# A transformer block on one core: the bias table's loads, its product and the pieces of one weight block are moved and recut

## The chip, the core and the metric

The kernel runs on one core of a Trainium2 chip. A core has five engines that run their own instruction streams and meet at semaphores: TensorE (PE, matrix products; its weight loads are listed as PEld), VectorE (DVE), ScalarE (ACT), GpSimd (POOL) and SyncE (SP). Data move between the memory outside the core and its own memory through 16 DMA engines. A transfer is issued by an instruction on SP, ACT or POOL. The metric is the time of one execution in device microseconds; the kernel before took 297.29 us (median of 3, 296.46 to 297.39).

## What is computed

One block for 256 tokens of width 1024, all in 32-bit floats:

```python
u = rms_norm(h, mix_norm_g[l])
proj = u @ w_in[l]
q, k, v, glu_a, glu_g = jnp.split(proj, splits, axis=-1)
attn_out = moba_attention(heads(q), heads(k), heads(v), rel_bias)
conv_out = conformer_conv(glu_a, glu_g, conv_w[l], conv_b[l], conv_ln_g[l], conv_ln_b[l])
mixed = jnp.concatenate([attn_out, conv_out], axis=-1)
h = h + mixed @ w_out[l]
u = rms_norm(h, ffn_norm_g[l])
h = h + (jax.nn.silu(u @ w_gate[l]) * (u @ w_up[l])) @ w_down[l]
return rms_norm(h, final_norm_g)
```

With 256 tokens there is one attention block of 256 keys, so attention is causal over all tokens, with 8 heads of 64. To each score a bias is added that depends on the head and on the distance of query and key: `rel_bias` is a table of 32 rows (buckets of distance) by 8 heads, and keys ahead of the query are masked. This bias is what the change is about.

## The kernel before

**Products in split parts.** Each 32-bit weight is split into an upper part `wh` (rounded to the matmul's fast 32-bit type, F32R) and a lower part `wl` (the raw value less `wh`); activations likewise. A product is three matmuls: upper by upper, upper by lower, lower by upper (`mm3`, `a_mm`). The upper part is made by `high` (ACT, or DVE for the pieces in `COPY_V`), the lower by `split` (DVE). Raw weights arrive in `raw` buffers of 128x1024, six in all, two to a block; `load` issues their DMAs on SP, one for each piece that `pieces` gives: halves of a block (1024 columns), or quarters (512 columns) for names in `FINE` (L37).

**Order.** All engines run in the order in which the program is traced (`keep_in_program_order`). Most of the first two thirds is a hand-written list, `PROGRAM` (L43 to L53), of steps that the table `ops` maps to functions. An engine's order is the order in which the steps give it instructions; where an instruction must wait, all behind it on that engine wait.

**Start.** Before the list runs, SP issues eight chunk pairs (L197 to L199): a 128x512 piece of the first weight block (`raw_a`, blocks `a0_0`, `a0_4`) and a 128x256 chunk of x (`xs`). POOL sets `ones`, issues the DMAs of the one-hot matrix `hot_s` and of the bias table `rbt` (L201, L202), sets constants, and issues the DMA of the late columns of the vector table `pv` (L216, taps of the convolution, not read before the convolution's weights are made). PE runs nine matmuls on `ones` to warm up.

**First products.** Steps `a0.0` to `a0.7` each take one chunk: ACT and DVE make `wh`, the two parts `us` of x, and `wl`, and PE runs 12 matmuls into `pa` and `pg`. Then `a1.0` to `a1.3` take the weight blocks `a1_0` and `a1_1`, two chunks each. Meanwhile `sq.*` adds up the squares of x (`accx`), `rs` turns them into the norm's factor (PE `ps_x`, DVE `ms_x`, POOL `rc_x`, DVE `dg_x`), and `rb` spreads it over the columns (PE `pb_x`). `glu.0` makes the convolution's input `upad`; `ud.0` writes it out (POOL), `us.0` reads it back four times, shifted (`ustk`, SP), for the matmuls `c.0.0` (`pc`).

**The bias.** `hot` is 33x384: for each of 384 distances a one-hot column (scaled) or, for masked ones, the 33rd row with the mask's value; `rbt` has the table in 32 rows and ones in the 33rd. `pz` (`bias_mm`, after `a0.0` in the list) multiplies them in plain F32 into 8x384, `zs` (ACT) copies the result out, `zd` (POOL) writes it to memory outside the core, and `bd` (SP, after `ld.qk1`) reads it into `bias`, each partition one column further on. The first reader is step `t.0` (`lg` on DVE).

Of the kernel before, what the change touches and what calls it, by code (L numbers as in the profile page):

```python
# [10 lines left out]
F32 = mybir.dt.float32  # L11
F32R = mybir.dt.float32r
# [17 lines left out]
MASK = 1e30  # L30
ZN = 384
# [2 lines left out]
ONV = TAPS - 4 * Q  # L34
UW = S + 32
LOOK = 2
FINE = ("a0_0", "a0_4")  # L37
COPY_V = (("a0_0", 0), ("a0_0", 1))
WARM = 9
SHIFT = 16  # L40
MIX = 48

PROGRAM = """  # L43
ld.a1_0 a0.0 pz a0.1 a0.2 a0.3 zs zd ld.a1_1 a0.4 a0.5 a0.6 a0.7 ld.qk0
w.a1_0.0 sq.0 sq.1 w.a1_0.1 sq.2 sq.3 sq.4 ld.qk1 bd a1.0 w.a1_1.0 sq.5 sq.6 sq.7 h.a1_1.1 h.qk0.0 h.qk0.1 a1.1 rs
w.a1_1.1 w.qk0.0 ld.qk2 a1.2 rb glu.0 ud.0 w.qk0.1 ld.v0 us.0 a1.3 w.qk1.0 w.qk1.1 glu.1 ud.1 us.1 ld.qk3
qk.0.0 qk.0.1 qo.0 cw.0 h.qk2.0 h.qk2.1 qk.1.0 sc.0 qk.1.1 w.qk2.0 t.0 w.qk2.1 ct.0.0.1 ld.v1 qo.1 c.0.0 h.v0.0 n.0 ct.0.1.3 sc.1 t.1 h.v0.1 ct.0.3.4 w.v0.0
c.0.1 fl.0 fo.0 n.1 h.qk3.0 ct.0.4.5 w.v0.1 w.qk3.0 qk.2.0 fl.1 fo.1 qk.2.1 ld.o0 ct.0.5.7 qo.2 h.qk3.1
v.0 cw.1 w.qk3.1 ld.o1 sc.2 t.2 v.1 h.v1.0 co.0 w.v1.0 qk.3.0 n.2 h.v1.1 w.v1.1 ld.o2 ct.1.0.2 fl.2 fo.2 qk.3.1 h.o0.0 w.o0.0 qo.3
# [5 lines left out]
PV_G1, PV_G2, PV_CB, PV_LG, PV_LB, PV_T = 0, 8, 16, 20, 24, 28  # L55
PV_CW = PV_T + CC * ONV
PV_FOLD = PV_CW + 16 * Q
PV_N = PV_FOLD + 32
# [3 lines left out]
def block_kernel(ctx, tc, xT, w_in, w_out, w_gu, w_down, pvec, gfin, relb, hot, out):  # L62
    nc = tc.nc
    const = ctx.enter_context(tc.tile_pool(name="const", bufs=1))
# [4 lines left out]
    w1 = ph1.enter_context(tc.tile_pool(name="w1", bufs=1))  # L69
# [3 lines left out]
    def mm(*args, **kw):  # L73
        return tc.keep_in_program_order(nc.tensor.matmul(*args, **kw))  # L74
# [12 lines left out]
    act, vec, pool, sync = (InOrder(e) for e in (nc.scalar, nc.vector, nc.gpsimd, nc.sync))  # L87

    def bank(i, name):
        return psum.tile([P, 512], F32, tag=f"b{i}", name=name)  # L90
# [86 lines left out]
    us = const.tile([P, KD * 2 * S + SHIFT], F32R, name="us")  # L177
# [3 lines left out]
    pv = const.tile([P, PV_N + 8], F32, name="pv")  # L181
# [2 lines left out]
    ident = const.tile([P, P], F32, name="ident")  # L184
    warm = const.tile([P, 1], F32, name="warm")
    accx = w1.tile([P, S], F32, name="accx")
    rbt = w1.tile([NB + 1, 32], F32, name="rbt")
    hot_s = w1.tile([NB + 1, ZN], F32, name="hot_s", tag="lg", bufs=2)
    upad = [w1.tile([P, 2 * UW + 4], F32, name=f"upad{i}", tag="pts", bufs=4) for i in range(2)]
    ustk = []  # L190
    wstk = [w1.tile([P, 8 * Q, 32], F32, name=f"wstk{i}", tag="wstk", bufs=2) for i in range(2)]
# [5 lines left out]
    for k in range(KD):  # L197
        next(first[k // 4])
        sync.dma_start(xs[:, k], xT[:, k * S : (k + 1) * S])  # L199
    pool.memset(ones, 1.0)  # L200
    pool.dma_start(hot_s, hot)  # L201
    pool.dma_start(rbt[0:NB, 0:H], relb)  # L202
    wm = bank(4, "wm")
    for i in range(WARM):
        mm(wm[:, 0:P], ones, ones, start=i == 0, stop=i == WARM - 1)
# [1 line left out]
    pool.affine_select(out=ident, in_=ident, compare_op=ALU.not_equal, fill=1.0, base=0,  # L207
                       pattern=[[-1, P]], channel_multiplier=1)
    pool.memset(mhalf, -0.5)
    pool.memset(rbt[NB : NB + 1, 0:H], 1.0)  # L210
    for t in upad:
        pool.memset(t[:, 0 : TAPS - 1], 0.0)
        pool.memset(t[:, TAPS - 1 + S : UW + TAPS - 1], 0.0)
        pool.memset(t[:, UW + TAPS - 1 + S :], 0.0)
    pool.memset(invc, 1.0 / (CC * P))
    pool.dma_start(pv[:, PV_T:PV_N], pvec[:, PV_T:])  # L216

    col = lambda lo, i: pv[:, lo + i : lo + i + 1]

# [66 lines left out]
    ud = [dram.tile([P, 2 * UW + 4], F32, name=f"ud{half}") for half in range(2)]  # L286
# [59 lines left out]
    rb = w1.tile([P, S], F32, name="rb")  # L346
# [3 lines left out]
        act.copy(rb, pb[:, :S])  # L350


    zs = w1.tile([H, ZN], F32, name="zs", tag="lg", bufs=2)
    zd = dram.tile([H, ZN], F32, name="zd")
    bias = w1.tile([P, H, S], F32, name="bias")

# [3 lines left out]

    pzs = []

    def bias_mm():
        pzs.append(bank(6, "pz"))
        mm(pzs[0][0:H, 0:ZN], rbt[:, 0:H], hot_s, start=True, stop=True)

    def bias_copy():
        act.copy(zs, pzs[0][0:H, 0:ZN])

    def bias_out():  # L370
        pool.dma_start(zd, zs)
# [161 lines left out]
    def a0(k):  # L533
# [3 lines left out]
        split(f"a0_{k // 4 * 4}", k % 4)  # L537
        a_mm(0, k, f"a0_{k // 4 * 4}", k % 4 * 512)

    ops = {"ld": fetch, "zd": bias_out, "bd": bias_in, "ud": stack_out, "us": stack_in, "h": high, "w": split, "rb": row_scale, "pz": bias_mm, "zs": bias_copy, "vt": v_out, "rs": scale_x,  # L540
           "a0": a0, "a1": a1, "glu": glu, "qk": qk_mm, "qo": qk_out, "sc": score, "t": logits, "n": normed, "fl": flip,
           "fo": flip_out, "v": v_mm, "pv": pv_mm, "mo": mix_out, "l": norm, "o": o_mm, "f": finish, "c": conv,
           "co": conv_out, "cw": conv_weights, "ct": conv_taps, "hs": lambda m: sumsq(acch, xs[:, m], m, "h"),
# [83 lines left out]
    hb = w2.tile([P, KD, KD, 32], F32, name="hb")  # L627
# [57 lines left out]
    a, b = FG - 2, FG - 1  # L685
    for t in range(2):
# [32 lines left out]
        sq = w2.tile([P, 512], F32, name=f"fsq{t}2", tag="fsq", bufs=2)  # L719
# [13 lines left out]
def _buckets():  # L733
    half = NB // 2
    d = np.arange(S)
    large = half + (np.log(np.maximum(d, 1) / half) / math.log(128 / half) * (NB - half) + 1e-9).astype(int)
    return np.where(d < half, d, np.minimum(large, NB - 1))


def _one_hot():  # L740
    hot = np.zeros((NB + 1, ZN), np.float32)
    b = _buckets()
    for n in range(ZN):
        dist = n - (P - 1)
        if 0 <= dist < S:
            hot[b[dist], n] = float(HD) ** 0.5
        else:
            hot[NB, n] = -MASK
    return hot

# [20 lines left out]
def _layout(x, mix_norm_g, w_in, rel_bias, conv_w, conv_b, conv_ln_g, conv_ln_b, w_out,  # L773
            ffn_norm_g, w_gate, w_up, w_down, final_norm_g):
    flat = lambda a: np.ascontiguousarray(a.reshape(P, -1))
    wi = _rows_d(w_in[0])
    q, k, v, a, g = (wi[:, :, i * 512 : (i + 1) * 512] for i in range(5))
    parts = []
    for half in range(2):
        c = slice(half * S, (half + 1) * S)  # L780
        parts.append(np.concatenate([a[:, :, c], g[:, :, c]], axis=2).reshape(P, -1))
    for hp in range(4):
        c = slice(hp * P, (hp + 1) * P)
        parts.append(np.concatenate([q[:, :, c], k[:, :, c]], axis=2).reshape(P, -1))
# [34 lines left out]
```

## Time and profile before

| what | value |
|---|---|
| three runs | 297.29 us median, 296.46 to 297.39 |
| the profiled execution | 296.92 us, of which the profile's span covers 295.0 |
| DVE, ACT, POOL busy | 203.3, 149.2, 44.2 us |
| DMA | 63.73 MB, mean 216 GB/s over the span |
| SP's own DMA queue (q1) | 54.80 MB, 57.2% of 16 engines |
| POOL's DMA queue (q0) | 8.08 MB, 9.7% |

The span runs from the first to the last instruction that the profile lists. "Busy" is the time in which an engine had at least one instruction under way. The chain of work that ended last is followed back from the last instruction; a step on it that gets shorter makes the kernel shorter, unless another chain is nearly as long. q1 is fed by SP and q0 by POOL; both end on the same 16 DMA engines, so the share of one is taken from what is left to the other.

### The profile page before, as it was taken

The numbers are of one execution on the slowest core, as the hardware profiler recorded it, in microseconds if no ns is written. First come the engines' busy times: TensorE is split into PE (matmuls) and PEld (weight loads), VectorE is DVE, ScalarE is ACT, GpSimd is POOL, SyncE is SP. The second block draws the span as 40 slices with busy tenths as digits, with TensorE's granted clock in tenths as the row PEclk, the third lists the DMA queues.
The fourth block names the chain that finished last, engine by engine and source line by source line (L and its number), as shares of the span: only waits on it lengthen the run. The fifth ranks groups of instructions, "written<-read, shape, count | busy, mean of one in ns | idle before, by whom it ended". The sixth has DMA issues, their size and how long they took to land.

```text
span 295.0 us, 4763 instructions
## 1 busy us (share of the span) xinstructions
PE 286.6 (97%) x1750; PEld 243.3 (82%) x1750; DVE 203.3 (69%) x373; ACT 149.2 (51%) x251; POOL 44.2 (15%) x83
## 2 busy tenths in 40 slices
PE   8999999999999999999999999999999999999991
PEld 6899987887689998888888888888888888888880
DVE  2887999888988689864975748282838466321894
ACT  2984554364583778634645454361718163402531
POOL 4000000000000000232231313321411313130000
PEclk9999999999999999999999999999999999999997
DMA  6999879945317455886998939979795959420022
GB/s 188 353 396 345 266 168 267 364 103 189 81 65 244 143 184 154 280 327 208 304 348 213 315 139 299 326 224 367 241 268 158 303 126 321 147 71 1 0 69 76
DMA packets 21624, 63.73 MB, mean 216 GB/s; under 512 B 3117, under 2 KB 5701, under 8 KB 21600
## 3 DMA queue, kind: packets, MB, share of 16 engines
q1 hardware_dynamic: 18176, 54.80, 57.2%
q0 software_dynamic: 2992, 8.08, 9.7%
q10 hardware_dynamic: 432, 0.54, 0.5%
q8 instruction: 14, 0.23, 0.3%
q14 instruction: 10, 0.08, 0.1%
HBM read 58.08 MB, written 5.32 MB: 215 GB/s over the span
## 4 chain that ended last, share of the span: by engine, by line
PE 92%; issue 2%; DMA 2%; DVE 2%; SPq 1%; ACT 0%; POOLq 0%; POOL 0%; DVEq 0%
PE pf L74 41%; PE pd L74 18%; PE pqk L74 8%; PE py L74 7%; PE pv L74 4%; PE pc L74 4%; PE pa L74 3%; PE pg L74 3%; DMA raw_a<-in_w_in 2%; PE pt L77 1%; PE ps L74 1%; PE po L74 1%; DVE ht L85 1%; SPq L85 1%; DVE hg L85 0%
## 5 line engine op out<-in xcount | busy, mean ns | idle before, releaser
L74 PE MATMUL pf<-wl,us 128*128 128x512 f32 x176 | 68.5, 389 | 0.0
L74 PE MATMUL pf<-wh_u,us 128*128 128x512 f32 x176 | 56.3, 390 | 0.0
L74 PE MATMUL pf<-wh_g,us 128*128 128x512 f32 x176 | 56.0, 389 | 0.0
L85 DVE TENSOR_TENSOR ff<-fs,pf 128x256 f32<-128x256 f32 x22 | 9.0, 418 | 53.0 <-ACT fs L85 53.0
L85 ACT ACTIVATE fs<-pf,rc_h 128x256 f32<-128x256 f32 x22 | 10.3, 474 | 65.2 <-PE pf L74 64.7
L74 PEld LDWEIGHTS pf<-wh_u,us 128*128 128x128 f32 x176 | 33.0, 188 | 6.9
L74 PEld LDWEIGHTS pf<-wh_g,us 128*128 128x128 f32 x176 | 33.0, 188 | 6.9
L74 PEld LDWEIGHTS pf<-wl,us 128*128 128x128 f32 x176 | 33.0, 188 | 6.7
L74 PE MATMUL pd<-wh_d,fh 128*128 128x512 f32 x84 | 32.9, 391 | 0.0
L74 PE MATMUL pd<-wh_d,fl 128*128 128x512 f32 x84 | 32.7, 389 | 0.0
L74 PE MATMUL pd<-wl,fh 128*128 128x512 f32 x84 | 32.7, 389 | 0.0
L85 DVE TENSOR_TENSOR wl<-raw_u,wh_u 128x1024 fp32r<-128x1024 f32 x22 | 26.4, 1219 | 6.0 <-ACT wh_u L85 6.0
L85 POOL DMA_DIRECT2D fb<-fd x40 | 23.2, 586 | 48.6 <-DMA fd<-fv 19.7
L85 ACT CAST wh_u<-raw_u 128x1024 fp32r<-128x1024 f32 x22 | 22.7, 1051 | 10.3 <-PE pf L74 8.0
L85 DVE TENSOR_TENSOR wl<-raw_g,wh_g 128x1024 fp32r<-128x1024 f32 x22 | 25.9, 1218 | 2.0 <-ACT wh_g L85 2.0
L85 DVE TENSOR_TENSOR wl<-raw_d,wh_d 128x1024 fp32r<-128x1024 f32 x22 | 25.6, 1203 | 0.5 <-ACT wh_d L85 0.5
L74 PE MATMUL pqk<-us,wh_qk 128*128 128x256 f32 x128 | 22.6, 280 | 0.0
L85 ACT CAST wh_g<-raw_g 128x1024 fp32r<-128x1024 f32 x22 | 21.9, 1046 | 0.0
L85 ACT CAST wh_d<-raw_d 128x1024 fp32r<-128x1024 f32 x22 | 21.9, 1047 | 0.0
L74 PEld LDWEIGHTS pqk<-us,wh_qk 128*128 128x128 f32 x128 | 19.4, 188 | 0.4 <-issue 0.3
L74 PEld LDWEIGHTS pd<-wh_d,fl 128*128 128x128 f32 x84 | 15.8, 188 | 3.3
L74 PEld LDWEIGHTS pd<-wh_d,fh 128*128 128x128 f32 x84 | 15.8, 188 | 3.2
(154 smaller groups left out, 527.1 us busy)
## 6 DMA issues: line engine op xcount, KB each, us to landing
raw_g<-in_w_gu SPq DMA_DIRECT2D x22, 512.0 KB, 5.5
raw_u<-in_w_gu SPq DMA_DIRECT2D x22, 512.0 KB, 6.7
raw_d<-in_w_down SPq DMA_DIRECT2D x22, 512.0 KB, 4.7
raw_qk<-in_w_in SPq DMA_DIRECT2D x8, 512.0 KB, 7.2
raw_o<-in_w_out SPq DMA_DIRECT2D x8, 512.0 KB, 3.7
fd<-fv POOLq DMA_DIRECT2D x10, 256.0 KB, 4.2
fb<-fd POOLq DMA_DIRECT2D x40, 64.0 KB, 5.4
ustk<-ud SPq DMA_DIRECT2D x8, 288.0 KB, 5.8
```

What stands on the lines that cost most here:

```text
L74: return tc.keep_in_program_order(nc.tensor.matmul(*args, **kw))
L77: return tc.keep_in_program_order(nc.tensor.transpose(o, i, ident))
L85: return lambda *a, **k: tc.keep_in_program_order(f(*a, **k))
```

## The change

The three edits named in the title. The one-hot matrix becomes 64x256: two copies of 32 rows, no mask row and only the 256 distances that count. It and the table (also twice, by a source pattern with a leading step of 0) are issued on SP behind the eight chunk pairs. The table is split into an upper part (rows 0 to 31 of `rbr`) and a lower part (rows 32 to 63), and one F32R matmul over 64 rows and 256 columns adds both. The mask is set beforehand by POOL in all of `zs`, and DVE copies the 256 columns into its middle. In the list, `pz` moves behind `a0.7`, with the new step `hb` (the splitting, on DVE) ahead of it; `zs` and `zd` move behind `sq.4`; `bd` moves behind `ld.qk2`. The DMA of `pv`'s late columns becomes the step `pl`. Block `a1_0` is loaded and split in four pieces instead of two.

```diff
-FINE = ("a0_0", "a0_4")
+FINE = ("a0_0", "a0_4", "a1_0")

 PROGRAM = """
-ld.a1_0 a0.0 pz a0.1 a0.2 a0.3 zs zd ld.a1_1 a0.4 a0.5 a0.6 a0.7 ld.qk0
-w.a1_0.0 sq.0 sq.1 w.a1_0.1 sq.2 sq.3 sq.4 ld.qk1 bd a1.0 w.a1_1.0 sq.5 sq.6 sq.7 h.a1_1.1 h.qk0.0 h.qk0.1 a1.1 rs
-w.a1_1.1 w.qk0.0 ld.qk2 a1.2 rb glu.0 ud.0 w.qk0.1 ld.v0 us.0 a1.3 w.qk1.0 w.qk1.1 glu.1 ud.1 us.1 ld.qk3
+ld.a1_0 a0.0 a0.1 a0.2 a0.3 ld.a1_1 a0.4 a0.5 a0.6 a0.7 hb pz ld.qk0
+w.a1_0.0 w.a1_0.1 sq.0 sq.1 w.a1_0.2 w.a1_0.3 pl sq.2 sq.3 sq.4 zs zd ld.qk1 a1.0 w.a1_1.0 sq.5 sq.6 sq.7 h.a1_1.1 h.qk0.0 h.qk0.1 a1.1 rs
+w.a1_1.1 w.qk0.0 ld.qk2 bd a1.2 rb glu.0 ud.0 w.qk0.1 ld.v0 us.0 a1.3 w.qk1.0 w.qk1.1 glu.1 ud.1 us.1 ld.qk3
...
-    rbt = w1.tile([NB + 1, 32], F32, name="rbt")
-    hot_s = w1.tile([NB + 1, ZN], F32, name="hot_s", tag="lg", bufs=2)
+    rbt = w1.tile([2 * NB, 24], F32, name="rbt")
+    rbr = w1.tile([2 * NB, H], F32R, name="rbr")
+    hot_s = w1.tile([2 * NB, S], F32, name="hot_s", tag="lg", bufs=2)
...
         sync.dma_start(xs[:, k], xT[:, k * S : (k + 1) * S])
+    sync.dma_start(hot_s, hot)
+    sync.dma_start(rbt[:, 0:H], bass.AP(tensor=relb.tensor, offset=relb.offset, ap=[[0, 2], [H, NB], [1, H]]))
     pool.memset(ones, 1.0)
-    pool.dma_start(hot_s, hot)
-    pool.dma_start(rbt[0:NB, 0:H], relb)
...
-    pool.memset(rbt[NB : NB + 1, 0:H], 1.0)
...
-    pool.dma_start(pv[:, PV_T:PV_N], pvec[:, PV_T:])
+    zs = w1.tile([H, ZN], F32, name="zs", tag="lg", bufs=2)
+    pool.memset(zs, -MASK)
+
+    def late_columns():
+        pool.dma_start(pv[:, PV_T:PV_N], pvec[:, PV_T:])
...
+    def bias_parts():
+        pzs.append(const.tile([2 * NB, S], F32R, name="hot_r", tag="sq", bufs=3))
+        vec.tensor_copy(pzs[0], hot_s)
+        vec.tensor_copy(rbr, rbt[:, 0:H])
+        low = slice(NB, 2 * NB)
+        vec.tensor_sub(rbr[low], rbt[low, 0:H], rbr[low].bitcast(F32))
+
     def bias_mm():
         pzs.append(bank(6, "pz"))
-        mm(pzs[0][0:H, 0:ZN], rbt[:, 0:H], hot_s, start=True, stop=True)
+        mm(pzs[1][0:H, 0:S], rbr, pzs[0], start=True, stop=True)

     def bias_copy():
-        act.copy(zs, pzs[0][0:H, 0:ZN])
+        vec.tensor_copy(zs[:, P - 1 : P - 1 + S], pzs[1][0:H, 0:S])
```

`_one_hot` builds the new matrix on the host; `bias_out` (`zd`) and `bias_in` (`bd`) themselves are as before.

More of the change, by code (lines that the diff above doesn't have):

```diff
@@ L350, in row_scale @@
         act.copy(rb, pb[:, :S])
-    zs = w1.tile([H, ZN], F32, name="zs", tag="lg", bufs=2)
     zd = dram.tile([H, ZN], F32, name="zd")
@@ L538, in a0 @@
         a_mm(0, k, f"a0_{k // 4 * 4}", k % 4 * 512)
-    ops = {"ld": fetch, "zd": bias_out, "bd": bias_in, "ud": stack_out, "us": stack_in, "h": high, "w": split, "rb": row_scale, "pz": bias_mm, "zs": bias_copy, "vt": v_out, "rs": scale_x,
+    ops = {"ld": fetch, "zd": bias_out, "bd": bias_in, "ud": stack_out, "us": stack_in, "h": high, "w": split, "rb": row_scale, "hb": bias_parts, "pl": late_columns, "pz": bias_mm, "zs": bias_copy, "vt": v_out, "rs": scale_x,
            "a0": a0, "a1": a1, "glu": glu, "qk": qk_mm, "qo": qk_out, "sc": score, "t": logits, "n": normed, "fl": flip,
@@ L740, in _one_hot @@
 def _one_hot():
[L741 to L749, printed above, removed]
+    hot = np.zeros((2, NB, S), np.float32)
+    hot[:, _buckets(), np.arange(S)] = float(HD) ** 0.5
+    return hot.reshape(2 * NB, S)
 def _conv_taps(w):
```

## The prediction

> **What bounds the kernel now.** First the page: busy times, then the chain that ended last.
>
> ```profile
> span 295.0 us, 4763 instructions
> ...
> PE 286.6 (97%) x1750; PEld 243.3 (82%) x1750; DVE 203.3 (69%) x373; ACT 149.2 (51%) x251; POOL 44.2 (15%) x83
> ...
> PE 92%; issue 2%; DMA 2%; DVE 2%; SPq 1%; ACT 0%; POOLq 0%; POOL 0%; DVEq 0%
> ```
>
> The chain is almost all PE. In order of time (start, length, what) it shows where that begins and ends:
>
> ```profile
> 2.59 5.38 DMA raw_a<-in_w_in
> ...
> 8.00 0.62 ACT wh_a L85
> ...
> 10.20 0.74 PE pa L74 x4
> ...
> 23.21 0.68 PE pg L74 x6
> 23.89 0.34 PE ps_x L74 x4
> 24.23 0.81 PE pa L74 x6
> ...
> 42.39 2.73 PE pc L74 x48
> ...
> 280.18 0.02 issue
> ```
>
> PE busy by windows says whether there is a hole in between (width, PE, PEld, DVE, ACT, POOL, clock, DMA share, GB/s):
>
> ```profile
> 10.20:280.20 270.00, 270.00 (x1657) 229.25 (x1658) 189.16 (x341) 140.64 (x233) 39.43 (x62) 1.00 0.70 223
> ```
>
> 270.00 of 270.00: PE does not wait from 10.20 to 280.20. So only three things can move the end: when this stretch starts, what PE work is put into it or taken out, and a new wait inside it. The tail behind 280.2 is not touched. The timeline of the start shows why the stretch doesn't begin earlier:
>
> ```profile
> 3.62 0.60 DVE L85 CAST wh_a<-raw_a 128x512 fp32r<-128x512 f32 x1 [2.75 <-DMA raw_a<-in_w_in]
> ...
> 6.71 0.81 PE L74 MATMUL pz<-hot_s,rbt 33*8 33x384 f32 x2
> ...
> 6.99 0.43 DVE L85 CAST wh_a<-raw_a 128x512 fp32r<-128x512 f32 x1 [1.01 <-DMA raw_a<-in_w_in]
> 7.33 0.51 ACT L85 ACTIVATE us<-xs,pv 128x256 fp32r<-128x256 f32 x1 [2.46 <-DMA xs<-in_xT]
> ...
> 7.89 0.39 PE L74 MATMUL pa<-us,wh_a 128*128 128x256 f32 x1 [0.37 <-ACT us L85]
> ...
> 10.20 0.39 PE L74 MATMUL pa<-us,wl 128*128 128x256 f32 x1 [0.21 <-DVE wl L85]
> ```
>
> The second weight piece arrives 3.4 us after the first (3.62 to 6.99), the second chunk of x at 7.33, the third piece at 7.97 (2.59 + 5.38). `pz` (0.81 us) sits in a hole that PE would have anyway: after it PE still idles 0.37 for x, then 0.21 for `wl`. **Taking `pz` out of that place therefore gains nothing by itself; earlier landings do**, and at most 0.81 + 0.37 + 0.21 = 1.4 us.
>
> **Start: the two loads leave POOL's queue.** The DMA queues in the windows 3 to 3.5 (one line), 3.5 to 4 (two) and 7 to 8 us (one): packets, MB, share of 16 engines.
>
> ```profile
> q0 software_dynamic: 3, 0.01, 27.6%
> ...
> q0 software_dynamic: 18, 0.03, 52.7%
> q1 hardware_dynamic: 43, 0.07, 42.1%
> ...
> q1 hardware_dynamic: 263, 0.36, 97.9%
> ```
>
> While the one-hot matrix moves on q0 it holds 27.6% and 52.7% of the engines for 0.5 us each: 0.14 + 0.26 = 0.40 us of all sixteen. SP's queue moves 43 packets in that half microsecond, against 263 / 2 = 131 in an undisturbed one. Behind the eight chunk pairs the matrix no longer stands ahead of chunk 1. Gain: 0.4 us. Against it stands the step `pl`:
>
> ```profile
> 1.32 0.71 POOL L85 DMA_DIRECT2D hot_s<-in_hot  x1 [0.38 <-issue]
> 2.03 0.54 POOL L85 DMA_DIRECT2D rbt<-in_relb  x1
> ...
> 3.87 0.59 POOL L85 DMA_DIRECT2D pv<-in_pvec  x1
> ...
> pv<-in_pvec POOLq DMA_DIRECT2D x1, 78.0 KB, 5.8
> rbt<-in_relb POOLq DMA_DIRECT2D x1, 1.0 KB, 3.8
> zd<-zs POOLq DMA_DIRECT2D x1, 12.0 KB, 6.2
> ```
>
> Its place in the list orders it only on POOL, which has nothing to wait for ahead of it. Nor do the readers of `pv` hold it: in the kernel before, `us` reads `pv`'s early columns while the late ones are under way (from 3.87 to 3.87 + 5.8 = 9.7), so the two parts are tracked apart. So I expect the columns not later but earlier: 3.87 - 0.71 - 0.54 = 2.6 us. Their 78 KB now compete with chunks 1 and 2: 0.078 MB at 0.36 MB per us is 0.2 us. Bounds for the start: a loss of 0.2 (the slow second piece has another cause, and the columns add to it) and a gain of 1.4 (the whole hole closes). I take a gain of 0.4, nearest to the row of q0; the columns cost part of it only if they hit the critical piece.
>
> **PE work put into the stretch.** `pz` now stands behind `a0.7`, where PE doesn't wait: one matmul of 256 columns. Six of 128x256 take 0.68 (23.21), so one is 0.11; the break of form after `ps_x` makes the next six 0.81, 0.13 more. Between 0.11 and 0.24: **+0.2**.
>
> **DVE's new work.** DVE feeds `accx`, and PE's `ps_x` at 23.89 needs it:
>
> ```profile
> 10.01 0.45 ACT L85 COPY zs<-pz 8x384 f32<-8x384 f32 x1
> ...
> 15.15 0.68 DVE L85 TENSOR_TENSOR wl<-raw_a,wh_a 128x512 fp32r<-128x512 f32 x1
> 16.58 1.22 DVE L85 TENSOR_TENSOR wl<-raw_a,wh_a 128x1024 fp32r<-128x1024 f32 x1 [0.75 <-ACT wh_a L85]
> ...
> 21.91 1.48 DVE L85 TENSOR_TENSOR accx<-accx,sq_x 128x256 f32<-128x256 f32 x3
> ```
>
> `accx` is done at 21.91 + 1.48 = 23.39, 0.5 us ahead of PE. `hb` (three small operations, at most 0.45 + twice 0.1 us by the copy of `zs` and by what is left of a small tile) falls into the 0.75 that DVE idles before 16.58. `zs` adds up to 0.45, the finer pieces 4 x 0.68 - 2 x 1.22 = 0.28: together 0.73. But the first `wl` of `a1_0` can start about 0.4 earlier, since its cast is half as long (0.62 at 8.00 for 512 columns). So `accx` comes some 0.3 later, inside the 0.5: cost 0. If that cover is gone, 0.2 to 0.5. ACT loses `zs` (0.45) and gains about as much in the four casts: 0, under PE.
>
> **The bias goes out late, and what follows it on SP.** `zs` moves from 10.0 to about 21 (behind `sq.4`), so `zd` lands near 21 + 6.2 = 27. SP meets `bd` behind the second `raw_qk` load of `ld.qk2`:
>
> ```profile
> bias<-zd SPq DMA_DIRECT2D x1, 1024.0 KB, 8.6
> ...
> 22.02 5.22 SPq L85 DMA_DIRECT2D raw_qk<-in_w_in  x2
> 28.05 4.02 SPq L85 DMA_DIRECT2D raw_v<-in_w_in  x2
> ...
> 34.66 1.37 SPq L85 DMA_DIRECT2D ustk<-ud  x3
> ...
> ustk<-ud SPq DMA_DIRECT2D x1, 288.0 KB, 6.1
> ...
> 39.65 0.28 DVE L85 CUSTOM_DVE_ANT_0 lg<-ps,bias 128x128 f32<-128x128 f32 x1
> ...
> 24.00:28.00 4.00, 4.00 (x35) 3.94 (x35) 2.89 (x6) 0.51 (x2) 0.72 (x1) 1.00 1.07 359
> 28.00:32.00 4.00, 4.00 (x36) 3.91 (x36) 3.77 (x9) 2.64 (x4) 0.62 (x1) 1.00 0.79 270
> ```
>
> Those two loads end at 22.02 + 5.22 = 27.24, so SP itself waits little. `bias` lands by 27.3 + 8.6 = 36, ahead of its reader at 39.65: cost 0. Its queue is another matter. Behind `bd` stand both loads of `v0` and then `us.0`; `ustk`'s last DMA is issued near 35.6 and lands 6.1 later, at 41.7, only **0.6-0.7 us ahead of the `pc` matmuls at 42.39**. The bias is 1.05 MB, 2.9 us at 359 GB/s. It moves from ahead of `qk2` to behind it; until the second `qk2` load is issued, at 26.9, only one `qk2` load (0.52 MB, 1.5 us) can fill its old place. So about 1.4 us come on top later, of which the idle DMA share of 28 to 32 (21% of 4 us, 0.8) takes up some, not all, as part of it is latency. I take 1.1 later against 0.6 of room: PE waits **0.5**. Ends: 0 (the idle share swallows it) and 2.9 - 0.6 = 2.3.
>
> Sum: -0.4 + 0.2 + 0 + 0.5 = **+0.3 us**. The profiled execution took 296.92, its span 295.0 and 1.9 around it; that is 0.4 below the median of 297.29. Added to the median: **297.6**.
>
> **What the skill says against one edit.** The Trainium skill, "DMA: Bandwidth & Descriptors", section "Rules for kernel authors", says that an access pattern whose outermost dimension is a small repeat count confines the DMA to that many engines; the table's source starts with a repeat of 2, so by it two engines would move 32 rows each. No row of before shows such a transfer, and its price here is in the third rival.
>
> **Rivals.**
> 1. *The hole at the start closes and `ustk` still lands in time.* For it: the second piece took 3.4 us, the next ones about one, and q0 was at work just then. Against: POOL's columns still come early. Price: -1.4 + 0.2 = -1.2: 296.1. Chance 0.22.
> 2. *`ustk` becomes the bound* (slower). Place: PE before `c.0.0`. If the bias delays `v0` and `ustk` by over 0.6 us, PE waits for each microsecond beyond; with little gain at the start (0.2) and 2.0 us of delay: -0.2 + 0.2 + 1.4 = +1.4: 298.7. For it: 0.6 us of room against 2.9 us of transfer; against: idle DMA share. Chance 0.18.
> 3. *The table lands late and DVE stands in `hb`*, with all `wl` of `a1_0` behind it. Before, 32 rows took 3.8 us to land; issued at about 11 behind the chunks, the table lands near 15 and is wanted at 15.8. It decides from 1 us later on; at 2 to 3 us late PE loses about 1.2 in all beyond the forecast: 298.8. Chance 0.06.
> 4. *The change doesn't do what it says at the start*: loads on another queue still use the same sixteen engines, and the columns fill the gap. Gain 0: +0.7: 298.0, within no change. Chance 0.12.
>
> **How the numbers follow.** Of this kernel a measurement can tell about 0.3% (0.9 us) from no change: 296.4 to 298.2 is "same". The forecast has 0.42. Same: 0.42 + 0.12 = 0.54; faster: 0.22; slower: 0.18 + 0.06 = 0.24. The range of 8 in 10 takes in most of the rivals on both sides: 296.0 to 299.0. By the bounds alone it could be -1.4 + 0.1 = -1.3 (296.0) to +0.2 + 0.24 + 0.5 + 2.3 = +3.2 (300.5); I cut the upper end, where all costs come together.
>
> **What would show it.** Start: the second piece's cast on DVE earlier than 6.99, PE's unbroken stretch earlier than 10.20, no `pz` before it. Columns: POOL's `pv` issue near 2.6 (if at 15 or later, I am wrong on `pl`). DVE: `accx` done ahead of `ps_x`, no idle PE there. Bias: `bias` issued after 27, and PE idle ahead of the first `pc` matmul with `ustk`'s DMA as releaser; if `pc` follows without a gap and the start has moved, rival 1 holds.

## The result, and the profile after

The changed kernel takes **301.03 us** (median of 6 runs, 299.61 to 302.43) beside 297.57 for the kernel before, measured with it (6 runs, 296.46 to 297.9): a ratio of **1.0115 [1.0088, 1.0141]**. It is slower, by 3.5 us; the forecast was 297.6 with a range up to 299.0. The profiled execution took 301.12, 4.2 more than the one of before, and its span of 299.3 is 4.3 longer.

The page of the changed kernel, with busy times and the chain's shares:

```profile
span 299.3 us, 4765 instructions
...
PE 287.5 (96%) x1749; PEld 244.2 (82%) x1749; DVE 204.1 (68%) x379; ACT 149.4 (50%) x252; POOL 43.3 (14%) x81
...
PE 85%; DVE 7%; issue 2%; DMA 2%; ACT 2%; POOL 0%; SPq 0%; POOLq 0%; DVEq 0%
```

PE's share of the chain falls from 92% to 85%, though PE is busy 0.9 us longer: part of what PE did without a break now stands behind other engines (DVE's 7% hang on the releaser that the profile names ahead of `pc`, see below). The chain, in order of time (start, length, what), says where:

```profile
10.19 0.73 PE pa L74 x4
...
18.40 0.21 PE pz L74
18.61 0.91 PE pa L74 x6
...
24.32 0.62 PE ps_x L74 x4
...
45.98 4.05 PE pc L74 x48
...
284.65 0.02 issue
```

Read it against the chain of before, piece by piece. The unbroken stretch starts at 10.19, before at 10.20: **nothing was won at the start**. `ps_x` starts at 24.32, before at 23.89: 0.43 later. The `pc` group starts at 45.98, before at 42.39, and takes 4.05 us for the same 48 matmuls, before 2.73. PE's last piece ends at 284.65, before at 280.18: 4.47 later.

The timeline of PE around that place (start, length, what, and in brackets the idle time before it and what ended it):

```profile
42.73 0.28 PE L74 MATMUL pqk<-us,wl 128*128 128x256 f32 x1
45.98 4.05 PE L74 MATMUL pc<-ustk,wstk 128*32 128x256 f32 x48 [2.98 <-DVE cacc L85]
```

PE stands still for **2.98 us** ahead of the first `pc`. The named releaser, `cacc`, is not what PE lacked: `pc` reads `ustk` and `wstk`, and two experiments with the same wait name the DMA of `ustk` (below). So the 4.47 us are: 0.43 up to `ps_x`, 0.19 more around it (`ps_x` itself took 0.62, before 0.34), 2.98 of waiting and 4.05 - 2.73 = 1.32 in a slow `pc` group, 4.92 in all, less about 0.45 that PE gets back by a shorter `pt` group near 65 to 70 us (0.66 us, before 1.14; experiment 2 says why).

**Why `ustk` is late.** SP's timeline, then what the landings took (KB, us from issue to landing), in the changed kernel:

```profile
28.00 0.43 SPq L85 DMA_DIRECT2D bias<-zd  x1
28.75 3.91 SPq L85 DMA_DIRECT2D raw_v<-in_w_in  x2
37.93 4.25 SPq L85 DMA_DIRECT2D ustk<-ud  x8
```

```profile
bias<-zd SPq DMA_DIRECT2D x1, 1024.0 KB, 7.8
...
ud<-upad POOLq DMA_DIRECT2D x1, 290.0 KB, 6.5
```

and the same for the kernel before, where the prediction did not look at `ud`:

```profile
34.27 11.02 SPq L85 DMA_DIRECT2D ustk<-ud  x8
```

```profile
ud<-upad POOLq DMA_DIRECT2D x1, 290.0 KB, 3.2
```

`ustk` is read back from `ud`, so SP can't issue it before `ud` has landed. `ud` is issued at 31.4 (before 31.0) and takes 6.5 us to land instead of 3.2: SP issues the first `ustk` 37.93 - 34.27 = 3.66 us later. The DMA queues of the changed kernel, in the windows 31.4 to 35 (one line) and 35 to 37.9 us (two), show what `ud` stood behind (packets, MB, share of 16 engines):

```profile
q1 hardware_dynamic: 877, 1.09, 98.3%
...
q1 hardware_dynamic: 216, 0.74, 64.4%
q0 software_dynamic: 80, 0.30, 25.0%
```

From 31.4 to 35 the SP queue holds all sixteen engines with the bias and `v0`; POOL's queue (q0), where `ud` is, moves no packet at all. All its 80 packets move once q1 thins out. In the kernel before, all 80 moved between 31.4 and 35, where the SP queue held 47.8%.

The windows from 24 us on, each of 4 us, say where that load comes from (columns as in the prediction: the last three are clock, DMA share and GB/s):

```profile
24.00:28.00 4.00, 3.97 (x34) 3.75 (x32) 2.46 (x6) 0.87 (x1) 0.73 (x1) 1.00 0.52 189
28.00:32.00 4.00, 4.00 (x36) 3.97 (x36) 3.79 (x8) 3.02 (x5) 0.57 (x1) 1.00 0.82 243
32.00:36.00 4.00, 4.00 (x37) 4.00 (x36) 3.90 (x8) 1.07 (x3) 0.04 (x1) 1.00 0.98 317
```

Before, 24 to 28 moved 359 GB/s at a share of 1.07; now it is 189 at 0.52. The bias has left that stretch, and nothing took its place. SP's waits in the window 26 to 28.4 us say why (us in total, times, longest):

```profile
SPq L85 <- DVE wl L85: 4.3, 1, 4.3
```

The second load of `qk2` waits 4.3 us for a buffer that DVE's split must free, and the bias stands behind it. It moves in 28 to 36 instead, and the stretch from 32 to 36 carries 317 GB/s where the kernel before had 254:

```profile
32.00:36.00 4.00, 4.00 (x37) 4.00 (x37) 3.79 (x8) 1.67 (x3) 0.00 (x0) 1.00 0.82 254
```

**One megabyte was shifted from a stretch in which nothing took its place into the one in which `ud` must cross.**

**Why the `pc` group is slow.** Windows of 1 us, PE, PEld, DVE, ACT, POOL, clock, DMA share, GB/s:

```profile
44.00:45.00 1.00, 0.00 (x0) 0.00 (x0) 0.96 (x5) 0.00 (x0) 0.00 (x0) 1.00 1.06 201
45.00:46.00 1.00, 0.02 (x3) 0.05 (x5) 1.00 (x4) 0.00 (x0) 0.00 (x0) 0.58 1.05 228
46.00:47.00 1.00, 1.00 (x12) 0.61 (x16) 0.73 (x2) 0.00 (x0) 0.00 (x0) 0.50 1.05 198
...
48.00:49.00 1.00, 1.00 (x18) 0.56 (x13) 0.00 (x0) 0.00 (x0) 0.00 (x0) 0.71 1.08 221
49.00:50.00 1.00, 1.00 (x22) 0.43 (x14) 0.00 (x0) 0.00 (x0) 0.00 (x0) 1.00 1.05 197
```

The granted clock is 0.50 from about 45.16 (0.58 in that window is 0.16 us at full and 0.84 at half) to about 48.58 (0.71 likewise): 3.4 us, of which PE works in the last 2.6, at half speed. That is 1.3 us, the same as the group's excess. So the wait is paid twice: once as a wait, and once as a lowered clock after it.

### The profile page after: what moved, and what is told of

It reads as the page before. It is cut to its first block, busy times and chain, and to the rows that moved or that the text cites. A ratio compares the mean times of both kernels' runs of the same rounds, so it can differ in the third digit from the quotient of the medians.

```text
span 299.3 us, 4765 instructions
## 1 busy us (share of the span) xinstructions
PE 287.5 (96%) x1749; PEld 244.2 (82%) x1749; DVE 204.1 (68%) x379; ACT 149.4 (50%) x252; POOL 43.3 (14%) x81
## 4 chain that ended last, share of the span: by engine, by line
PE 85%; DVE 7%; issue 2%; DMA 2%; ACT 2%; POOL 0%; SPq 0%; POOLq 0%; DVEq 0%
PE pf L74 40%; PE pd L74 17%; PE py L74 7%; PE pc L74 4%; PE pv L74 4%; PE pqk L74 4%; DVE wl L85 3%; PE pa L74 2%; PE pg L74 2%; DMA xs<-in_xT 2%; PE pt L77 1%; PE po L74 1%; PE ps L74 1%; DVE ht L85 1%; ACT wh_qk L85 1%
## 5 line engine op out<-in xcount | busy, mean ns | idle before, releaser
L85 ACT ACTIVATE fs<-pf,rc_h 128x256 f32<-128x256 f32 x22 | 10.4, 475 | 64.9 <-PE pf L74 64.5
L74 PEld LDWEIGHTS pd<-wl,fh 128*128 128x128 f32 x84 | 15.8, 188 | 3.2
```

Of the source, the lines that this page charges most:

```text
L85: return lambda *a, **k: tc.keep_in_program_order(f(*a, **k))
```

## The experiments

Two theories stood at the outset. **A**: the late bias read alone does it, through `ud`, the late `ustk` and the lowered clock; the other parts cost little. **B**: the rest of the change (the new start, `pz` inside the stretch, DVE's added work) carries the loss. Two more are about the start alone. **E**: POOL's first DMA holds up the loads there. **F**: they arrive slowly whoever issues them. The other letters are explained where they stand.

### 1. The bias read moved, and nothing else

On the kernel before:

```diff
-w.a1_0.0 sq.0 sq.1 w.a1_0.1 sq.2 sq.3 sq.4 ld.qk1 bd a1.0 w.a1_1.0 sq.5 sq.6 sq.7 h.a1_1.1 h.qk0.0 h.qk0.1 a1.1 rs
-w.a1_1.1 w.qk0.0 ld.qk2 a1.2 rb glu.0 ud.0 w.qk0.1 ld.v0 us.0 a1.3 w.qk1.0 w.qk1.1 glu.1 ud.1 us.1 ld.qk3
+w.a1_0.0 sq.0 sq.1 w.a1_0.1 sq.2 sq.3 sq.4 ld.qk1 a1.0 w.a1_1.0 sq.5 sq.6 sq.7 h.a1_1.1 h.qk0.0 h.qk0.1 a1.1 rs
+w.a1_1.1 w.qk0.0 ld.qk2 bd a1.2 rb glu.0 ud.0 w.qk0.1 ld.v0 us.0 a1.3 w.qk1.0 w.qk1.1 glu.1 ud.1 us.1 ld.qk3
```

> The kernel before with one edit: the read of the bias (bd) is issued behind both loads of qk2, and nothing else. Theory A (the late bias fills the queue ahead of ud.0 and ustk): PE waits 2 to 3.5 us ahead of the first pc matmuls, these run slowly after the wait, and the time is 3 to 4.5 us above the kernel before (ratio 1.010 to 1.015). Rival B (the loss comes from the new start, pz inside PE's unbroken stretch and DVE's added work): within 0.5 us of the kernel before, no wait ahead of pc. Rival C (the later zd is needed for it, as zd's landing holds SP): little or nothing, since zd lands at 17 here.

Measured: 302.77 us, ratio 1.0194 [1.0168, 1.022]. That is 5.7 us more than before, and more than the whole change costs. PE's timeline and the landing of `ud`, in that kernel:

```profile
45.25 5.35 PE L74 MATMUL pc<-ustk,wstk 128*32 128x256 f32 x48 [3.11 <-DVE cacc L85]
```

```profile
ud<-upad POOLq DMA_DIRECT2D x1, 290.0 KB, 6.1
```

The wait (3.11) and the excess of the `pc` group (5.35 - 2.73 = 2.62) come to 5.7; the two profiled spans differ by 5.2. One moved step gives the whole effect: A holds as to its cause, though not as to its size, which lies above the 3 to 4.5 us expected. `zd` leaves as early as before in this kernel (10.4 us), so a later `zd` is not needed for it, and rival C is out.

### 2. The change without the bias read

This kernel leaves out the read of the bias table: a constant tile of zeros takes its place, so neither bias nor causal mask is added to the scores.

```diff
+    bias = w1.tile([P, H, S], F32, name="bias")
+    pool.memset(bias, 0.0)
...
-        sync.dma_start(bias, bass.AP(tensor=zd.tensor, offset=zd.offset, ap=[[1, P], [ZN, H], [1, S]]))
+        pass
```

> The changed kernel without the read of the bias: the tile is set to zero by POOL at the start, so the attention has no bias and no mask; all else, the write zd too, stays. Theory A: without that 1 MB ud.0 lands about 3.2 us after its issue and ustk in time; PE doesn't wait ahead of pc; what is left is pz and ps_x, 0.3 to 0.8 us above the kernel before. Rival B: a wait of over 2 us stays, so the bias is not its cause.

Measured: 296.83 us (10 runs), ratio 0.997 [0.9949, 0.9991]. PE does not wait ahead of `pc`; `ud` lands in 3.9 us and `ustk` is issued at 35.18. A's wait is gone, but its remainder of 0.3 to 0.8 us is not seen in the time. The profile shows why. `pc` starts at 42.82, before at 42.39, so the rest of the change does cost some 0.4 us up to there, after a start 0.17 earlier (10.03). That delay ends at the `pt` group, of the kernel before:

```profile
65.02 1.14 PE pt L77 x6
66.15 2.76 PE pqk L74 x24
```

and of this kernel:

```profile
65.49 0.66 PE pt L77 x6
66.14 2.76 PE pqk L74 x24
```

The six `pt` matmuls read `p`, which DVE has done at 65.66 before and at 65.50 here. In the kernel before PE stands there for some 0.5 us, inside a group that is listed as busy, and a PE that comes that much later loses nothing. So all else that the change does, `hb`, `pz` inside the stretch, DVE's copy, the finer pieces, shows no cost in the time. The kernel also moves 1 MB less than either, so its 0.3% is not a gain of the change, and a small cost could hide behind it; the third kernel of experiment 3, which moves every byte, sets the bound.

### 3. The way back: `v0` behind `us.0`, and the bias earlier

Three kernels on the changed one. First the loads of `v0` go behind `us.0`, so that SP holds them back until `ud` has landed:

```diff
-w.a1_1.1 w.qk0.0 ld.qk2 bd a1.2 rb glu.0 ud.0 w.qk0.1 ld.v0 us.0 a1.3 w.qk1.0 w.qk1.1 glu.1 ud.1 us.1 ld.qk3
+w.a1_1.1 w.qk0.0 ld.qk2 bd a1.2 rb glu.0 ud.0 w.qk0.1 us.0 ld.v0 a1.3 w.qk1.0 w.qk1.1 glu.1 ud.1 us.1 ld.qk3
```

> The changed kernel with the load of v0 issued behind us.0 instead of ahead of it. Theory A: ud.0 then meets only the bias in the queue and ustk goes ahead of 1 MB of v0, so ustk's last part lands 2 to 3 us earlier; the wait ahead of pc falls from 3.0 to under 1 us, the slow clock goes with it, and the time is 0.5 to 1.5 us above the kernel before. Rival B: no change against the changed kernel (3.5 us above). Rival D (the write ud.0 itself is slow, whatever stands behind it): the wait falls by under 1 us.

Measured: 298.43 us, ratio 1.0044 [1.002, 1.0069]. `ud` lands in 4.9 us, `ustk` is issued at 36.26, PE waits 1.3 us ahead of `pc`, and the group takes 2.80: at 1.3 us the clock is not lowered. Some six tenths of the loss are gone. The time is in A's range; the wait is a little above the 1 us that A allowed, and it fell by more than rival D did.

Second, the bias goes out earlier: `zs zd` right behind the first two pieces of `a1_0`, and `bd` back ahead of `ld.qk2`:

```diff
-w.a1_0.0 w.a1_0.1 sq.0 sq.1 w.a1_0.2 w.a1_0.3 pl sq.2 sq.3 sq.4 zs zd ld.qk1 a1.0 w.a1_1.0 sq.5 sq.6 sq.7 h.a1_1.1 h.qk0.0 h.qk0.1 a1.1 rs
-w.a1_1.1 w.qk0.0 ld.qk2 bd a1.2 rb glu.0 ud.0 w.qk0.1 ld.v0 us.0 a1.3 w.qk1.0 w.qk1.1 glu.1 ud.1 us.1 ld.qk3
+w.a1_0.0 w.a1_0.1 sq.0 sq.1 zs zd w.a1_0.2 w.a1_0.3 pl sq.2 sq.3 sq.4 ld.qk1 bd a1.0 w.a1_1.0 sq.5 sq.6 sq.7 h.a1_1.1 h.qk0.0 h.qk0.1 a1.1 rs
+w.a1_1.1 w.qk0.0 ld.qk2 a1.2 rb glu.0 ud.0 w.qk0.1 ld.v0 us.0 a1.3 w.qk1.0 w.qk1.1 glu.1 ud.1 us.1 ld.qk3
```

> The changed kernel with zs and zd right behind the first two pieces of a1_0, and bd ahead of qk2 as in the kernel before. Theory A: zd is issued near 19 and lands near 24, the bias moves in the place where it moved before, ustk lands in time and PE doesn't wait ahead of pc: 0.3 to 0.9 us above the kernel before, which is pz inside the stretch (0.4) and the later ps_x (0 to 0.4). Rival B: 3 us or more above the kernel before, as the start and DVE's work are as in the changed kernel. Rival C: SP now waits for zd ahead of qk2, qk2 lands late and PE waits ahead of qk.2.

Measured: 300.52 us, ratio 1.0102 [1.0062, 1.0141]. The expectation of A missed. SP's timeline in that kernel says why:

```profile
20.11 0.33 SPq L85 DMA_DIRECT2D raw_qk<-in_w_in  x1
24.78 0.39 SPq L85 DMA_DIRECT2D bias<-zd  x1
25.26 2.43 SPq L85 DMA_DIRECT2D raw_qk<-in_w_in  x2
```

SP reaches `bd` just after 20 but stands there until 24.78, when `zd` has landed; meanwhile it issues nothing, and the two `qk2` loads come behind the bias. The place in the list was earlier, but the queue ran dry (a DMA share of 0.32 from 24 to 25 us and 0.12 from 25 to 26) and the same volume followed: `ud` took 5.8 us, PE waited 2.39 and the `pc` group took 4.49. What counts in these kernels is not where the read stands in the list but how much is under way when `ud` must cross.

Third, both edits together.

> The changed kernel with both repairs: zs, zd and bd early as in e4_bias_early, and v0 behind us.0 as in e2_v0_behind_us. Theory A: ud.0 meets neither the whole bias nor v0; the wait ahead of pc is 0 to 0.5 us at a full clock; 0.2 to 0.8 us above the kernel before, of which 0.4 is pz in the stretch. Rival D (the write ud.0 is slow by itself, whatever is behind it): the wait stays near 1.3 as in e2_v0_behind_us.

Measured: 297.73 us (10 runs), ratio 1.0 [0.9983, 1.0016]. `ud` lands in 3.6 us, `ustk` is issued at 35.04, there is no wait ahead of `pc`. The loss is gone and nothing is won: a repaired version of the change equals the kernel before, within 0.2% either way. The 0.2 to 0.8 us that A left for the rest of the change are at the limit of that and not seen.

### 4. Is the slow `pc` group the clock?

On the changed kernel, 12 matmuls of 128x128 on constants (listed as 24) keep PE at work during the wait; they are added work.

```diff
+KEEP = 12
...
+        if half == 0 and j == 0:
+            keep = bank(3, "keep")
+            for i in range(KEEP):
+                mm(keep[:, 0:P], ones, ones, start=i == 0, stop=i == KEEP - 1)
```

> The changed kernel with 12 matmuls of 128x128 on ones into an idle bank ahead of the first pc matmuls; they wait for nothing of the transfers and take about 2.5 us of the 3.0 that PE waits there. Theory G (part of the loss is PE's clock, granted at half after the wait): the granted clock stays at 1.00 over 43 to 50 us, the 48 pc matmuls take 2.7 to 2.8 instead of 4.05, and the time falls by 1.2 to 1.5 us against the changed kernel, to 1.5 to 2.5 above the kernel before, although the kernel does more. Rival H (pc is slow as its later data arrive one by one): pc still takes 4, and the time stays or rises.

Measured: 300.26 us, ratio 1.0091 [1.0057, 1.0125]. That kernel's timeline of PE:

```profile
42.77 2.84 PE L75 MATMUL keep<-ones 128*128 128x128 f32 x24
45.84 2.80 PE L75 MATMUL pc<-ustk,wstk 128*32 128x256 f32 x48 [0.23 <-DMA ustk<-ud]
```

`ustk` comes just as late (the group starts at 45.84, in the changed kernel at 45.98), but the same 48 matmuls take 2.80, not 4.05, and the clock is 1.00 in every window from 43 to 50 us. So the slow group is the clock's, and the idle time lowers it. The last wait names its releaser: the DMA of `ustk`. As to size, PE is through the group 1.4 us earlier than in the changed kernel (48.64 against 50.03), while the ratios differ by 0.24%, 0.7 us, with intervals that overlap; expected were 1.2 to 1.5. So the clock's part is shown in the profile, and in the medians only in its direction.

### 5. The late columns and the start

On the changed kernel, `pl` moves behind `zd`, and POOL issues nothing at the start:

```diff
-w.a1_0.0 w.a1_0.1 sq.0 sq.1 w.a1_0.2 w.a1_0.3 pl sq.2 sq.3 sq.4 zs zd ld.qk1 a1.0 w.a1_1.0 sq.5 sq.6 sq.7 h.a1_1.1 h.qk0.0 h.qk0.1 a1.1 rs
+w.a1_0.0 w.a1_0.1 sq.0 sq.1 w.a1_0.2 w.a1_0.3 sq.2 sq.3 sq.4 zs zd pl ld.qk1 a1.0 w.a1_1.0 sq.5 sq.6 sq.7 h.a1_1.1 h.qk0.0 h.qk0.1 a1.1 rs
```

> The changed kernel with the late columns of pv really late: their DMA stands behind zd on POOL, which waits for zs until 22 us, so POOL issues no DMA during the start. Theory E (POOL's first DMA, whatever it carries, holds up the loads at the start): the second x chunk lands 0.5 to 1.3 us earlier than 7.4, PE's unbroken stretch starts at 9 to 9.7 instead of 10.2. Theory F (the loads start slowly by themselves, POOL's queue is only a bystander): the second chunk at 7.0 to 7.4 and the stretch within 0.3 us of 10.2. The wait ahead of pc stays in both, so the time stays 2 to 4 us above the kernel before.

Measured: 299.42 us, ratio 1.0092 [1.0067, 1.0116]. The second x chunk is taken up at 6.87, as E expected, and the stretch starts at 9.76, 0.4 earlier than in the changed kernel: outside F's range, and just outside E's. One profile does not decide it: in experiment 1, with POOL's loads at the start, they come at 6.61 and 9.87. The wait ahead of `pc` stays, and in PE's list of waits it is named (us in total, times, longest):

```profile
PE pc L74 <- DMA ustk<-ud: 2.9, 1, 2.9
```

On the kernel before, the columns alone go late (POOL then issues them behind `zd`, at 11.38):

```diff
-    pool.dma_start(pv[:, PV_T:PV_N], pvec[:, PV_T:])
...
+        pool.dma_start(pv[:, PV_T:PV_N], pvec[:, PV_T:])
```

> The kernel before with one edit: the DMA of pv's late columns is issued on POOL behind zd, so near 11 us instead of 3.9; the one-hot matrix and the table stay where they were. Theory E (POOL's DMAs slow the start): the columns no longer compete with chunks 2 and 3; PE's unbroken stretch starts up to 0.3 us earlier than in the kernel before, time 0 to 0.3 us less, near the limit of what can be told. Theory F (a bystander): the start lies between 9.8 and 10.2 as in the two profiles seen with the same start (10.20 and 9.87), no difference in time.

Measured: 298.14 us (12 runs), ratio 1.0014 [0.9991, 1.0036]: no difference, and a start at 10.33. Over all profiles, the stretch starts between 9.87 and 10.33 in the ten that have a POOL load at the start (median 10.17), and at 9.67, 9.76, 9.90 and 10.15 in the four that have none (the kernel with POOL's bias below, the first of this section, and the two of 3 with the early bias). These are single profiles of different kernels, and the two groups overlap; their medians differ by about 0.3 us. So POOL's traffic may account for some 0.3 us of the start, but not for the slow second piece, which comes between 5.9 and 7.1 us in all of them. Why it does stays open.

### 6. The parts without the bias's move

Finer pieces of `a1_0` alone, on the kernel before:

```diff
-FINE = ("a0_0", "a0_4")
+FINE = ("a0_0", "a0_4", "a1_0")
...
-w.a1_0.0 sq.0 sq.1 w.a1_0.1 sq.2 sq.3 sq.4 ld.qk1 bd a1.0 w.a1_1.0 sq.5 sq.6 sq.7 h.a1_1.1 h.qk0.0 h.qk0.1 a1.1 rs
+w.a1_0.0 w.a1_0.1 sq.0 sq.1 w.a1_0.2 w.a1_0.3 sq.2 sq.3 sq.4 ld.qk1 bd a1.0 w.a1_1.0 sq.5 sq.6 sq.7 h.a1_1.1 h.qk0.0 h.qk0.1 a1.1 rs
```

> The kernel before with one edit: a1_0 is loaded and split in four pieces. Theory: PE never waits for a1_0 in either kernel, so the time is that of the kernel before within 0.3 us; the first cast of a1_0 starts 0.3 to 0.7 us earlier than 15.5, as half as much has to land, and accx is done within 0.3 us of 23.4. Rival: the two extra DMAs hold SP's queue, the first piece lands no earlier, accx is done after 24 and PE waits for it ahead of ps_x, up to 0.5 us.

Measured: 296.71 us (10 runs), ratio 0.9971 [0.9954, 0.9988]. It is the fastest kernel of the study, 0.3% below the kernel before, at the edge of what can be told; its profiled span is 295.0, the same as before. `accx` is done at 22.70, before at 23.39. That does not shorten a path on which PE did not wait. So the theory missed: the time is 0.9 us lower and `accx` 0.7 us earlier, where it allowed 0.3 for each; the rival, a later `accx`, is not seen either.

The whole bias without a one-hot product, on the kernel before: POOL writes the 256 columns from the table (laid out as 8x32) in 18 small operations, there is no `pz`, and the columns of `pv` go late.

```diff
-ld.a1_0 a0.0 pz a0.1 a0.2 a0.3 zs zd ld.a1_1 a0.4 a0.5 a0.6 a0.7 ld.qk0
+ld.a1_0 a0.0 a0.1 a0.2 a0.3 zd ld.a1_1 a0.4 a0.5 a0.6 a0.7 ld.qk0
...
+    act.dma_start(rbt, relb)
...
+    pool.memset(zs, -MASK)
+    pool.tensor_scalar(zs[:, P - 1 : P - 1 + NB // 2], rbt[:, 0 : NB // 2], float(HD) ** 0.5, None, op0=ALU.mult)
+    for bk, lo, hi in _runs()[NB // 2 :]:
+        for at in range(lo, hi, P):
+            n = min(hi - at, P)
+            pool.tensor_scalar(zs[:, P - 1 + at : P - 1 + at + n], ones[0:H, 0:n], rbt[:, bk : bk + 1], float(HD) ** 0.5, op0=ALU.mult, op1=ALU.mult)
```

> The kernel before without the one-hot product: the table comes as 8 rows of 32 (1 KB, on ACT's queue), and POOL writes the 256 columns of the bias in 18 small operations (one for the 16 exact buckets, one or two for each of the others) straight into zs; zd and bd as before, the late columns of pv behind rc_x. No hot matrix, no product on PE, no copy. By the runs so far: bias and ustk in their old places, so no wait ahead of pc; no POOL DMA in the first 6 us, so PE's unbroken stretch starts at 9.8 to 10.2; nothing added to the stretch. 0 to 0.5 us less than the kernel before, that is 0.998 to 1.000, no more than can just be told. Rival: POOL's small operations take over 10 us and zd goes out after 14; then the bias lands a little later, still ahead of its reader, and the time is as before.

Measured: 297.48 us (12 runs), ratio 1.0003 [0.9979, 1.0027]: no difference. That kernel's timeline of POOL:

```profile
4.33 11.63 POOL L85 TENSOR_SCALAR zs<-ones,rbt 8x3 f32<-8x3 f32 x17
16.26 0.76 POOL L85 DMA_DIRECT2D zd<-zs  x1 [0.31 <-POOL zs L85]
```

Seventeen operations of 8 rows take 11.63 us, 0.68 each, so `zd` leaves at 16.26, SP issues the bias at 21.66 instead of 19.86, and PE waits 0.9 us ahead of `pc`, where none was expected; the time is as the rival had it. What the missing `pz` may have freed is not seen in the time.

Two last kernels ask whether `ustk`'s room in the kernel before was itself too small, so that `v0` behind `us.0` would help there, alone and with the finer pieces.

```diff
-w.a1_1.1 w.qk0.0 ld.qk2 a1.2 rb glu.0 ud.0 w.qk0.1 ld.v0 us.0 a1.3 w.qk1.0 w.qk1.1 glu.1 ud.1 us.1 ld.qk3
-qk.0.0 qk.0.1 qo.0 cw.0 h.qk2.0 h.qk2.1 qk.1.0 sc.0 qk.1.1 w.qk2.0 t.0 w.qk2.1 ct.0.0.1 ld.v1 qo.1 c.0.0 h.v0.0 n.0 ct.0.1.3 sc.1 t.1 h.v0.1 ct.0.3.4 w.v0.0
+w.a1_1.1 w.qk0.0 ld.qk2 a1.2 rb glu.0 ud.0 w.qk0.1 us.0 ld.v0 a1.3 w.qk1.0 w.qk1.1 glu.1 ud.1 us.1 ld.qk3
+qk.0.0 qk.0.1 qo.0 cw.0 h.qk2.0 h.qk2.1 qk.1.0 sc.0 qk.1.1 w.qk2.0 t.0 w.qk2.1 ct.0.0.1 ld.v1 qo.1 c.0.0 n.0 ct.0.1.3 sc.1 t.1 h.v0.0 h.v0.1 ct.0.3.4 w.v0.0
```

> The kernel before with the load of v0 issued behind us.0, and the first cast of v0 on ACT moved behind the exponentials of t.1, so that it doesn't wait for the later load. Theory A2 (the kernel before already has too little room for ustk: in some of its executions PE waits up to 2 us ahead of pc, which is its spread of 296.3 to 299.3): ustk lands 1 to 2 us earlier, the runs lie closer together (within 1.5 us), ratio 0.996 to 0.998, as for e9_before_fine, whose bias left SP 0.7 us earlier. Rival K (the gain of e9_before_fine has to do with DVE or ACT, not with ustk): ratio 1.000, the spread stays.

> Both edits on the kernel before: a1_0 in four pieces, and v0 behind us.0. Theory A2: the two give the same room, so together little more than either, ratio 0.996 to 0.998. Rival K: as e9_before_fine (0.997) whatever e11_before_v0_behind shows.

Measured: 297.73 us, ratio 1.0008 [0.9984, 1.0032], alone, and 297.57 us, ratio 0.9993 [0.9973, 1.0012], with the finer pieces (12 runs each). Neither gains, although `ustk` is issued at 33.42 and 33.76, 0.85 and 0.5 us earlier than before. The runs lie closer together (297.08 to 298.55 and 297.13 to 298.15) than the 23 of the kernel before that were measured with them (296.07 to 299.3), which would fit a room for `ustk` that is sometimes used up; that is argued, not shown. And the 0.3% of the finer pieces did not come back here, so its cause, and whether it lasts, stay open.

## Why the prediction was wrong

**The bias goes out late (the step that failed).** The place and the wait were right: PE stands ahead of the first `pc` for `ustk`, as in the second rival. Its size was not: 0.5 us forecast, 2.3 as the upper bound, 2.98 measured, and 1.32 more for the clock. Two things were missed.

- I put the bias's bytes ahead of `ustk` alone. `ustk` is the second of two transfers in a row: `ud` must first land, on another queue but through the same sixteen engines. That first transfer went from 3.2 to 6.5 us, and it moved `ustk`'s issue by 3.66 us. With the room of about 0.65 and the 0.62 that PE itself comes later this gives 3.66 - 0.65 - 0.62 = 2.4 of wait; the other 0.6 is the read itself. I let idle engine time between 28 and 32 us take up part of the bias. It hardly did: that stretch carries no more than before (243 GB/s at a share of 0.82, before 270 at 0.79), and the added load came in the stretch behind, from 32 to 36 us.
- I priced a wait as a wait, and so put the clock behind it at nothing. The windows after it show half the clock for 3.4 us, and experiment 4 shows that the idle time is the cause. A wait of 3 us cost 4.3.

The reading under it, 270.00 of 270.00 and so no wait, was too strict as well: the `pt` group at 65.02 holds some 0.5 us of waiting (experiment 2), which took back part of the delay.

**The start.** A gain of 0.4 was forecast, and 0 came, as in the fourth rival. These rows are from the timeline of the changed kernel:

```profile
2.25 0.74 POOL L85 DMA_DIRECT2D pv<-in_pvec  x1
...
6.35 0.43 DVE L85 CAST wh_a<-raw_a 128x512 fp32r<-128x512 f32 x1 [0.33 <-DMA raw_a<-in_w_in]
...
7.43 0.51 ACT L85 ACTIVATE us<-xs,pv 128x256 fp32r<-128x256 f32 x1 [2.54 <-DMA xs<-in_xT]
```

That the columns come earlier was right (2.25, forecast near 2.6). The second weight piece does come 0.64 earlier (6.35, before 6.99), but the second chunk of x does not (7.43, before 7.33), and it is x that `pa` waits for. The first sign that I named was the weight piece, though x ended PE's wait already before. Where both came earlier, the stretch did start earlier: 5.99 and 6.61 in experiment 1, with a start at 9.87. The Trainium skill says in "DMA: Bandwidth & Descriptors", section "Issuing engines are not separate DMA queues", that all issuers feed the same engines; that the start stayed where it was agrees with it (10.19 against 10.20), but does not prove it.

**`pz` in the stretch.** Forecast +0.2, with 0.24 at most; measured 0.21 for `pz` and 0.23 for the six matmuls behind it (0.91 instead of 0.68): 0.44. My upper bound, 0.11 for the matmul and 0.13 for the group behind it, had both terms, but each is nearly twice as large. I took the one from a row of like matmuls and the other from the break after `ps_x`; that the change of form costs more at `pz` is argued, and no run takes it apart.

**DVE's new work.** Forecast: `accx` 0.3 later, inside a room of 0.5. From DVE's and ACT's timelines:

```profile
15.37 0.28 DVE L85 CAST hot_r<-hot_s 64x256 fp32r<-64x256 f32 x1
15.57 0.16 DVE L85 CAST rbr<-rbt 64x8 fp32r<-64x8 f32 x1
15.76 0.16 DVE L85 TENSOR_TENSOR rbr<-rbt,rbr 32x8 fp32r<-32x8 f32 x1
...
22.80 1.47 DVE L85 TENSOR_TENSOR accx<-accx,sq_x 128x256 f32<-128x256 f32 x3
```

```profile
16.28 1.28 ACT L85 CAST wh_a<-raw_a 128x512 fp32r<-128x512 f32 x2 [1.95 <-DMA raw_a<-in_w_in]
```

`hb` is about as long as forecast, 0.55, and waits for nothing, so the third rival, a late table, is not seen. But `accx` is done at 24.27, 0.88 later than before, and the room is gone: PE's `ps_x` follows at 24.32, and its group takes 0.62 instead of 0.34. The pieces of `a1_0` come later, not earlier: SP issues the first at 11.36 (before 10.34), behind the one-hot matrix and the table that it now also issues, and ACT casts at 16.28 (before 15.50). In the kernels of experiments 2 and 4, which start alike, the first cast comes at 15.14 and 14.77, earlier than before, and `accx` is still late (24.10 and 24.19). There ACT waits for the last piece, and casts it at 18.51 and 18.60; before, its second half came at 17.14. I had counted the new DMAs for what they carry, not as two instructions ahead of the next weights on SP. By experiment 2 this shows no price in the end.

## What to carry to other kernels

Before a large transfer is moved later, list all that must cross the engines behind it, and follow chains of transfers (write out, wait, read back) link by link: here the write was slowed most, though it stood on another queue. A stretch that the move leaves empty is lost if the loads behind it wait for buffers. And a new wait on PE is to be priced with the clock behind it: here 2.39 us were enough to lower it, and 1.3 us were not. A busy share of 100% does not say that an engine never waits.

## What the runs showed of the hardware

**The lowered clock comes in pieces of 3.4 us.** Besides the changed kernel, three experiments waited long enough; these are the windows of 1 us in which their clock changes (columns as above, the clock third from the end). The bias read alone (1):

```profile
44.00:45.00 1.00, 0.00 (x0) 0.00 (x0) 1.00 (x4) 0.00 (x0) 0.00 (x0) 0.55 1.04 226
...
50.00:51.00 1.00, 1.00 (x12) 0.48 (x6) 0.00 (x0) 0.00 (x0) 0.00 (x0) 0.54 1.03 373
```

The late columns on the changed kernel (5):

```profile
44.00:45.00 1.00, 0.00 (x0) 0.00 (x0) 1.00 (x4) 0.00 (x0) 0.00 (x0) 0.83 1.07 237
...
48.00:49.00 1.00, 1.00 (x21) 0.54 (x16) 0.00 (x0) 0.00 (x0) 0.00 (x0) 0.97 1.08 205
```

The early bias (3, the second):

```profile
45.00:46.00 1.00, 0.88 (x16) 0.66 (x20) 1.00 (x4) 0.00 (x0) 0.00 (x0) 0.96 1.10 214
...
49.00:50.00 1.00, 1.00 (x14) 0.47 (x8) 0.00 (x0) 0.00 (x0) 0.00 (x0) 0.84 1.00 242
```

Worked out as above, half clock lasts from 44.10 to 50.92, from 44.66 to 48.06, and from 45.92 to 49.32: 6.8, 3.4 and 3.4 us, beside 3.4 in the changed kernel. It begins 2.0 to 3.2 us after PE fell idle, in the last case even 0.8 us after PE was at work again; a wait of 1.3 us lowered nothing. The Trainium skill, "TensorE: Matmul & The Clock Gate", section "Part 1: The HAM clock gate", tells of an activity window of about 3.4 us that runs freely, and of half clock after an idle one. The 3.4 us agree. Its rule in "Why this matters for your kernels", no idle gap over about 3 us between bursts, is too mild here: a gap of 2.39 us was enough.

**A transfer on POOL's queue can stand still beside a full SP queue.** `ud` moved no packet in the 3.6 us from 31.4 to 35 while q1 had 98.3% of the engines. The Trainium skill, "DMA: Bandwidth & Descriptors", section "Queues, rings and completion order", says that an engine goes round the queues that have work, packet by packet; by that alone some of the 80 packets should have moved. Whether its descriptors were not yet there or the engines passed it over, no run here shows.
